# Second-type MLPs: up projections of 18 of 22 pairs as seven products of quarter matrices, with the weight sums made by DMA in the first block

## The chip, the core and the metric

The kernel runs on one core of a Trainium2 chip. The metric is the device time of one execution in microseconds. TensorE (PE) multiplies, with its weight loads shown as PEld; VectorE (DVE), ScalarE (ACT) and GpSimd (POOL) do the elementwise work; SyncE (SP) issues DMAs, and ACT and POOL can issue them too.

## The reference, cut to what matters

A sequence of 512 tokens with 1024 channels goes through one block of a first type and two layers of a second type. The change concerns the MLP that closes each second-type layer:

```python
    for l in range(DEPTH_2):
        ...
        h2 = _rmsnorm(x, g_ffn[l])
        z = _dwconv(h2 @ w_up[l].astype(h2.dtype), w_dw_ffn[l], b_dw_ffn[l])
        zg, zv = jnp.split(z, 2, axis=-1)
        x = x + (jax.nn.silu(zg) * zv) @ w_down[l].astype(h2.dtype)
    return _rmsnorm(x, g_final)
```

w_up is 1024 x 5632 (2816 gate columns, then 2816 value columns), w_down 2816 x 1024; _dwconv is a convolution of three taps over the tokens, for each column by itself.

## The kernel before

**Layout.** x stays on the chip, transposed: 8 tiles of 128 channels x 512 tokens. A projection into 128 output columns is a sum over 8 input tiles. Every fp32 number is used as a high and a low part, so each 128x128 weight block costs three matmuls (mm3, L380 to L382: high x high, high weight x low input, low weight x high input) of 512 columns into one PSUM bank.

**Weights** are packed by the host into units of 8 blocks (512 KB), in the order of use, and streamed by prep and take: a DMA on SP's queue into raw (3 buffers), a cast on ACT into whi (L359), a subtraction on POOL into wlo (L360), 4 buffers each. take starts a unit's chain three units ahead of PE (AHEAD = 3). The engines are in-order queues; the order on each is set by a scheduler, with hand-made queue-order edges through issue_behind.

**The second-type MLP.** 22 pairs (128 gate and 128 value columns) go in two chunks of 11 (CHUNK2). The first four projections of a layer (two pairs) are made "outer": input tile by input tile, as x becomes ready (proj_outer). Behind them fin makes the RMS factor r: a matmul with ones over the squares (total, L480), ACT and DVE steps (rsqrt, L344, L489 to L491). Then each pair takes two PSUM banks of the pool's eight; conv3 multiplies a bank by r (L1289, DVE), starts the conv with a scaled copy (L1292, ACT) and adds two shifted terms (L1293, L1294, DVE); silu (L344, ACT), the product gate x value (L1308, DVE) and the split into ah (L448, ACT) and al (L449, DVE) follow. After a chunk's 11 pairs, 8 down projections of 11 blocks are added to x (L1313, DVE). norm_in, ahead of the MLP, makes xh and xl of x (L451, ACT; L452, DVE) and sums squares (L463).

**The end.** final makes the last two down projections in halves of 256 columns, the last norm (total, L480, and rsqrt) for each half, and the outputs o (L1348, DVE and POOL), each half's as soon as its factor is there.

**The first block** has an attention of eight heads, in which ACT, DVE and PE alternate, then its gates and its own MLP.

## Time and profile before

| | |
|---|---|
| median of 3 runs | 1880.58 us (1879.77 to 1882.03) |
| profiled execution | 1880.29 us, of it span 1878.6 us |
| PE busy | 1839.2 us, 98% of the span |
| DVE, ACT, POOL busy | 958, 946, 938 us (51%, 50%, 50%) |
| second-type MLP, first layer | 923.7 to 1283.4 us |
| second-type MLP, second layer | 1505.7 to 1867 us |

Shares are averages over stages. The chain of waits puts 89% of the span on PE. In the two MLP stages PE never idles; everywhere else its gaps are short.

### The profile page before, as it was taken

How to read it: one execution, taken by the hardware profiler on the slowest of the kernel's cores; microseconds unless marked ns; L12 is line 12 of the kernel's file. 1: busy time of each engine (PE TensorE's matmuls, PEld its weight loads, DVE VectorE, ACT ScalarE, POOL GpSimd, SP SyncE). 2: the span in 40 equal slices, each digit the busy share in tenths (PEclk: the TensorE clock that was granted, in tenths of full speed). 3: DMA queues.
4: the chain of work that ended last, by engine and by line, in shares of the span. 5: the costliest groups of instructions: out<-in, count | busy, mean ns of one | idle time of the engine just before them, and what ended most of it. 6: DMA issues, size and time to landing. Idle time of an engine off the chain costs nothing.

```text
span 1878.6 us, 22097 instructions
## 1 busy us (share of the span) xinstructions
PE 1839.2 (98%) x8448; PEld 1495.8 (80%) x8448; DVE 958.1 (51%) x1420; ACT 946.3 (50%) x1442; POOL 938.4 (50%) x510
## 2 busy tenths in 40 slices
PE   8999999999999999999999999999999999999997
PEld 6877888888888888766888888888866788888886
DVE  4666552724022037997565225522898565405543
ACT  6766633643243347697554224433778554314442
POOL 5233444644444557866644444454966464444442
PEclk9999999999999999999999999999999999999999
DMA  5111223222222222200222222222210122222221
GB/s 188 68 57 62 79 101 135 93 94 101 92 99 98 94 90 71 98 29 21 94 106 95 97 101 91 101 101 90 91 51 23 64 99 101 101 91 101 100 91 56
DMA packets 48649, 164.89 MB, mean 88 GB/s; under 512 B 5536, under 2 KB 7584, under 8 KB 48544
## 3 DMA queue, kind: packets, MB, share of 16 engines
q1 hardware_dynamic: 46304, 160.34, 24.3%
q10 hardware_dynamic: 2240, 3.15, 0.5%
q8 instruction: 66, 1.08, 0.2%
q14 instruction: 39, 0.32, 0.1%
HBM read 161.37 MB, written 2.10 MB: 87 GB/s over the span
## 4 chain that ended last, share of the span: by engine, by line
PE 89%; DVE 6%; ACT 3%; issue 1%; POOL 1%; DMA 0%; SPq 0%; DVEq 0%; ACTq 0%; POOLq 0%
PE b L381 23%; PE b L382 23%; PE b L380 23%; PE mm L381 3%; PE s L1140 3%; PE mm L380 3%; PE mm L382 3%; PE t L1157 2%; DVE xl L452 1%; PE av L1162 1%; PE av L1163 1%; PE cv L480 1%; ACT whi L359 1%; DVE x L650 1%; PE b L480 1%
## 5 line engine op out<-in xcount | busy, mean ns | idle before, releaser
L360 POOL TENSOR_TENSOR wlo<-raw,whi 128x1024 fp32r<-128x1024 f32 x300 | 720.9, 2405 | 809.9 <-ACT whi L359 809.6
L359 ACT CAST whi<-raw 128x1024 fp32r<-128x1024 f32 (+1 forms) x302 | 313.6, 1040 | 506.4 <-PE b L381 414.6
L380 PE MATMUL b<-xh,whi 128*128 128x512 f32 (+1 forms) x1296 | 495.4, 382 | 2.7 <-ACT xh L451 2.7
L381 PE MATMUL b<-xl,whi 128*128 128x512 f32 (+1 forms) x1296 | 491.4, 379 | 3.4 <-DVE xl L452 3.4
L382 PE MATMUL b<-xh,wlo 128*128 128x512 f32 (+1 forms) x1296 | 491.1, 379 | 0.0
L381 PEld LDWEIGHTS b<-xl,whi 128*128 128x128 f32 x1296 | 244.1, 188 | 51.9 <-DVE xl L452 4.2
L380 PEld LDWEIGHTS b<-xh,whi 128*128 128x128 f32 x1296 | 244.2, 188 | 50.5 <-ACT xh L451 3.1
L382 PEld LDWEIGHTS b<-xh,wlo 128*128 128x128 f32 x1296 | 244.1, 188 | 45.6
L380 PE MATMUL b<-ah,whi 128*128 128x512 f32 (+1 forms) x646 | 243.6, 377 | 0.0
L381 PE MATMUL b<-al,whi 128*128 128x512 f32 (+1 forms) x646 | 243.2, 377 | 0.0
L382 PE MATMUL b<-ah,wlo 128*128 128x512 f32 (+1 forms) x646 | 243.2, 376 | 0.0
L381 PEld LDWEIGHTS b<-al,whi 128*128 128x128 f32 x646 | 121.6, 188 | 22.4
L380 PEld LDWEIGHTS b<-ah,whi 128*128 128x128 f32 x646 | 121.5, 188 | 22.4
L382 PEld LDWEIGHTS b<-ah,wlo 128*128 128x128 f32 x646 | 121.6, 188 | 22.0
L1228 POOL TENSOR_TENSOR cacc<-cacc,pd 128x510 f32<-128x510 f32 (+14 forms) x94 | 119.8, 1275 | 26.6 <-ACT pd L1226 22.8
L1212 DVE SCALAR_TENSOR_TENSOR cv<-u,vec,cv 128x497 f32<-128x497 f32 (+13 forms) x146 | 108.2, 741 | 8.4 <-ACT cv L1202 6.5
L1289 DVE TENSOR_TENSOR b<-b,r 128x512 f32<-128x512 f32 x88 | 61.0, 697 | 97.3 <-PE b L382 97.1
L1313 DVE TENSOR_TENSOR x<-x,b 128x512 f32<-128x512 f32 x30 | 20.6, 687 | 161.3 <-PE b L382 161.3
L448 ACT CAST ah<-cg 128x512 fp32r<-128x512 f32 x44 | 27.3, 621 | 98.7 <-DVE cg L1308 98.7
L380 PE MATMUL mm<-xh,whi 128*128 128x512 f32 x176 | 69.3, 394 | 0.0
L871 DVE TENSOR_TENSOR b<-rl,b 128x512 f32<-128x512 f32 x32 | 22.1, 696 | 92.5 <-ACT rl L870 92.5
L381 PE MATMUL mm<-xl,whi 128*128 128x512 f32 x176 | 68.7, 391 | 0.0
(430 smaller groups left out, 2851.0 us busy)
## 6 DMA issues: line engine op xcount, KB each, us to landing
raw<-w SPq DMA_DIRECT2D x295, 512.0 KB, 3.2
x<-xT SPq DMA_DIRECT2D x8, 256.0 KB, 6.5
x<-xT ACTq DMA_DIRECT2D x8, 256.0 KB, 4.8
raw<-w SPq DMA_DIRECT2D x7, 256.0 KB, 2.6
outT<-o ACTq DMA_DIRECT2D x4, 256.0 KB, 2.4
outT<-o SPq DMA_DIRECT2D x4, 256.0 KB, 2.5
vec<-vec SPq DMA_DIRECT2D x1, 363.0 KB, 6.9
f<-pos SPq DMA_DIRECT2D x1, 256.0 KB, 3.3
```

What stands on the lines that cost most here:

```text
L359: nc.scalar.copy(out=hi[:, cs], in_=raw[:, cs])
L360: (eng or nc.gpsimd).tensor_tensor(out=lo[:, cs], in0=raw[:, cs], in1=hi[:, cs].bitcast(F32), op=ALU.subtract)
L380: mm(ps, lhsT=wb[0], rhs=xb[0], start=start, stop=False, **kw)
L381: mm(ps, lhsT=wb[0], rhs=xb[1], start=False, stop=False, **kw)
L382: mm(ps, lhsT=wb[1], rhs=xb[0], start=False, stop=stop, **kw)
L448: nc.scalar.copy(out=hi, in_=src)
L480: self.nc.tensor.matmul(full[:, :n], lhsT=self.ones, rhs=a, start=i == 0, stop=i == len(parts) - 1)
L1140: mm(s, lhsT=q[:, qb * P : (qb + 1) * P], rhs=k, start=True, stop=True)
L1157: nc.tensor.transpose(pt[:, qb * P : (qb + 1) * P], probs[qb][:, t * P : (t + 1) * P], self.ident)
L1212: ins = V.scalar_tensor_tensor(out=acc[:, o], in0=us[i][:, u], scalar=self.v("w_dw_conv_2", l, i * CONV_K + k), in1=acc[:, o], op0=ALU.mul ...
L1228: G.tensor_tensor(out=acc[:, o], in0=acc[:, o], in1=pd, op=ALU.add)
L1289: V.tensor_tensor(out=ps, in0=ps, in1=r, op=ALU.mult)
```

## The change

**Seven products.** Take a pair's 256 x 1024 weights as quarters, gate or value columns against the first or second four input tiles (a11, a12: gate; a21, a22: value), and the normed input as quarters B11, B12, B21, B22: first or second four tiles against the first or second 256 tokens. Pairs 0 to 3 of each layer stay plain; for pairs 4 to 21 the two banks are made of seven products of a weight quarter (or sum S1 to S4) with an input quarter (or difference T1 to T4), each 4 blocks x 3 matmuls of 256 columns, with copies (snap, ACT) and additions (plus, DVE) of half banks between. A pair has 84 matmuls of 256 columns in place of 48 of 512. The value half comes out with its sign turned, for which the conv uses weights negated at the start (wneg).

**Inputs.** quarter_inputs writes the seven input operands once per layer. The norm factor goes into them, so total moves from behind the outer projections to behind their first three input tiles, and pairs 4 to 21 lose their multiply by r. hp, the pool of its temporaries, is closed before the conv tiles' pool is opened.

**Weights.** A new host array wq holds the quarters, rearranged only. S1 to S4 are made on the device in DRAM: 40 copies on ACT's queue and 40 accumulating additions on POOL's, of 1 MB each (0.5 MB for one region in five), issued one or two behind the casts (or the subtractions) of units 8 to 99. In before those units run from 37 to 600 us. In the quarter phase a unit arrives as two or three DMAs instead of one.

**Chunks and end.** Three chunks of 7, 7 and 8 pairs. The last two products of a chunk's last pair are interleaved with its first three down projections. In final, the first half's outputs come behind the second half's factor; those of tiles 4 to 7 on DVE behind the last addition to x.

```diff
-CHUNK2 = 11
+CHUNKS2 = (0, 7, 14, 22)
+PLAIN2 = 4
+OUTER2 = 2
+NDOWN = 3
+SUM_PAIRS = 4
+SUMS = ("S1", "S2", "S3", "S4")
+QUARTERS = ("a11", "a12", "a21", "a22")
+SIDE = {u: 2 if 10 <= u < 27 else 1 if u < 41 or u % 2 else 0 for u in range(8, 120)}
...
+        for _ in range(SIDE.get(u, 0)):
+            if self.side:
+                begin, on_pool = self.side.popleft()
+                self.issue_behind(begin(), rest if on_pool else cast)
...
+        for name, base, more in (("S1", "a21", "a22"), ("S3", "a11", "a21"), ("S2", "S1", "a11"), ("S4", "S2", "a12")):
+            for l in range(NL):
+                for g, r in enumerate(regs):
+                    self.side.append((copy(self.sum_of[l, name, g], self.sum_of[l, base, g] if base in SUMS else quarter(l, base, r)), False))
+            for l in range(NL):
+                for g, r in enumerate(regs):
+                    self.side.append((add(self.sum_of[l, name, g], quarter(l, more, r)), True))
...
+                if k == OUTER_LAG + 2 and between is not None:
+                    between()
...
+        op_ = tc.tile_pool(name="quarters", bufs=1, side="right", reuse_waits="tile")
+        ops = self.quarter_tiles(op_.__enter__())
+        hp_ = tc.tile_pool(name="hp", bufs=1, reuse_waits="tile")
+        hp = hp_.__enter__()
+        rs = []
+        def norms():
+            rs.append(fin(pp, "b", True))
+            self.quarter_inputs(hp, ops, "g_ffn_2", l, rs[0][1])
+        pss = self.proj_outer(pp, "b", acts, 2 * OUTER2, between=norms)
+        pss += [self.proj(pp, "b", acts) for _ in range(2 * (PLAIN2 - OUTER2))]
+        r = rs[0][0]
+        self._close(hp_)
+        self._close(xg)
+        ffc = tc.tile_pool(name="ffc", bufs=max(len(ks) for ks in chunks2()), reuse_waits="tile")
...
+                for f in ks:
+                    if f >= PLAIN2:
+                        break
+                    pg, pv = pss[2 * f : 2 * f + 2]
+                    for ps in (pg, pv):
+                        V.tensor_tensor(out=ps, in0=ps, in1=r, op=ALU.mult)
+                    a.append(unit(f, pg, pv, self.v("w_dw_ffn_2", l, 3 * (NF2 + f), 3)))
+                def snap(ps):
+                    t = fp.tile([P, S // 2], F32, name="snap", bufs=4)
+                    with tc.high_priority():
+                        A.copy(out=t, in_=ps)
+                    return t
+                def plus(out, a, b):
+                    with tc.high_priority():
+                        V.tensor_tensor(out=out, in0=a, in1=b, op=ALU.add)
+                def times(ps, name, start, stop):
+                    hi, lo = ops[name]
+                    for kk in range(KT // 2):
+                        self.mm3(ps, self.take(), (hi[:, kk], lo[:, kk]), start and kk == 0, stop and kk == KT // 2 - 1, skip_group_check=True)
+                def p4(g):
+                    times(g["v"][:, L], "T4", False, True)
+                    plus(g["v"][:, R], g["g"][:, R], g["u3"])
+                def p3(g):
+                    times(g["g"][:, R], "B22", False, True)
+                    plus(g["g"][:, R], g["g"][:, R], g["u2"])
+                    a.append(unit(g["f"], g["g"], g["v"], self.wneg[l][:, 3 * g["f"] : 3 * g["f"] + 3]))
+                old = None
+                for f in ks:
+                    if f < PLAIN2:
+                        continue
+                    g = {"f": f, "v": pp.tile([P, S], F32, name="b"), "g": pp.tile([P, S], F32, name="b")}
+                    times(g["v"][:, L], "B11", True, False)
+                    u1 = snap(g["v"][:, L])
+                    times(g["g"][:, L], "B21", True, True)
+                    plus(g["g"][:, L], g["g"][:, L], u1)
+                    if old is not None:
+                        p4(old)
+                    times(g["v"][:, L], "T2", False, False)
+                    g["u2"] = snap(g["v"][:, L])
+                    times(g["g"][:, R], "T1", False, False)
+                    if old is not None:
+                        p3(old)
+                    times(g["v"][:, L], "T3", False, False)
+                    g["u3"] = snap(g["v"][:, L])
+                    old = g
+                ds = [pp.tile([P, S], F32, name="b") for _ in range(NDOWN)]
+                def down(n0, n1):
+                    for n in range(n0, n1):
+                        k, m = divmod(n, NDOWN)
+                        self.mm3(ds[m], self.take(), a[k], k == 0, k == len(ks) - 1)
+                down(0, 4)
+                p4(old)
+                down(4, 8)
+                p3(old)
+                down(8, NDOWN * len(ks))
+                tail = 2 if l == NL - 1 and c == last_chunk else 0
+                for m in range(KT - tail):
+                    ps = ds[m] if m < NDOWN else self.proj(pp, "b", a)
+                    V.tensor_tensor(out=self.x[m], in0=self.x[m], in1=ps, op=ALU.add)
+                if tail:
+                    self.final(pp, a)
...
+    def quarter_inputs(self, pool, ops, gname, l, r):
+        nc = self.nc
+        V, A, G = nc.vector, nc.scalar, nc.gpsimd
+        L, R = HALVES
+        for k in range(0, KT // 2, 2):
+            h = []
+            for k0 in (k, KT // 2 + k):
+                t = pool.tile([P, 2, S], F32, name=f"h{len(h)}")
+                for j in range(2):
+                    V.scalar_tensor_tensor(out=t[:, j], in0=self.x[k0 + j], scalar=self.v(gname, l, k0 + j), in1=r, op0=ALU.mult, op1=ALU.mult)
+                h.append(t)
+            (b11, b12), (b21, b22) = ((t[:, :, L], t[:, :, R]) for t in h)
+            def put(name, src, eng):
+                hi, lo = (t[:, k : k + 2] for t in ops[name])
+                A.copy(out=hi, in_=src)
+                eng.tensor_tensor(out=lo, in0=src, in1=hi.bitcast(F32), op=ALU.subtract)
+            def temp():
+                return pool.tile([P, 2, S // 2], F32, name="t", bufs=3)
+            put("B11", b11, G)
+            put("B21", b21, G)
+            t1 = temp()
+            V.tensor_tensor(out=t1, in0=b11, in1=b12, op=ALU.subtract)
+            t2 = temp()
+            V.scalar_tensor_tensor(out=t2, in0=t1, scalar=-1.0, in1=b22, op0=ALU.mult, op1=ALU.subtract)
+            put("T2", t2, V)
+            put("T1", t1, V)
+            t3 = temp()
+            V.tensor_tensor(out=t3, in0=b22, in1=b12, op=ALU.subtract)
+            put("T3", t3, V)
+            V.scalar_tensor_tensor(out=t2, in0=t2, scalar=-1.0, in1=b21, op0=ALU.mult, op1=ALU.subtract)
+            put("T4", t2, V)
+            put("B22", b22, G)
...
         def norm(cs):
+            factor(cs)
+            if cs.start:
+                outputs(HALVES[0], added[cs.start])
+                outputs(cs)
...
+                    if behind is not None and j >= KT // 2 and not on_pool:
+                        self.issue_behind(ins, behind)
```

At the end of the plain projections, DVE before and now (b: PSUM banks with their numbers, cg and cv: conv tiles of gate and value, r: the norm factor). Before, where the first layer's MLP begins:

```order
L491 SCALAR_TENSOR_TENSOR r_7992<-b_7993,r_7992 128x512
L1289 TENSOR_TENSOR b_7868<-b_7868,r_7992 128x512
L1289 TENSOR_TENSOR b_7869<-b_7869,r_7992 128x512
L1289 TENSOR_TENSOR b_7870<-b_7870,r_7992 128x512
L1293 SCALAR_TENSOR_TENSOR cg_8002<-b_7868,vec_67,cg_8002 128x511
L1293 SCALAR_TENSOR_TENSOR cv_8007<-b_7869,vec_67,cv_8007 128x511
L1294 SCALAR_TENSOR_TENSOR cg_8002<-b_7868,vec_67,cg_8002 128x511
L1294 SCALAR_TENSOR_TENSOR cv_8007<-b_7869,vec_67,cv_8007 128x511
L1293 SCALAR_TENSOR_TENSOR cg_8019<-b_7870,vec_67,cg_8019 128x511
L1308 TENSOR_TENSOR cg_8002<-cg_8002,cv_8007 128x512
```

Now, at the same layer; b_8011 and b_8012 are pair 0's gate and value, b_8294 is the eighth and last plain bank:

```order
L1439 TENSOR_TENSOR b_8199<-b_8199,r_8063 128x512
L1439 TENSOR_TENSOR b_8230<-b_8230,r_8063 128x512
L1439 TENSOR_TENSOR b_8262<-b_8262,r_8063 128x512
L1439 TENSOR_TENSOR b_8294<-b_8294,r_8063 128x512
L1417 SCALAR_TENSOR_TENSOR cg_8335<-b_8011,vec_67,cg_8335 128x511
L1417 SCALAR_TENSOR_TENSOR cv_8339<-b_8012,vec_67,cv_8339 128x511
L1418 SCALAR_TENSOR_TENSOR cg_8335<-b_8011,vec_67,cg_8335 128x511
L1418 SCALAR_TENSOR_TENSOR cv_8339<-b_8012,vec_67,cv_8339 128x511
L1417 SCALAR_TENSOR_TENSOR cg_8352<-b_8013,vec_67,cg_8352 128x511
L1426 TENSOR_TENSOR b_8011<-b_8011,cv_8339 128x512
L1418 SCALAR_TENSOR_TENSOR cg_8352<-b_8013,vec_67,cg_8352 128x511
L554 TENSOR_TENSOR al_8347<-b_8011,ah_8346 128x512
```

Before, three multiplies stood ahead of the first conv; now all eight multiplies stand ahead of the first conv.

ACT in the same place, before:

```order
L344 ACTIVATE r_7992<-b_7993,epst_122 128x512
L344 ACTIVATE r_7992<-r_7992,lna1024_124 128x512
L340 ACT_TABLE_LOAD
L1292 ACTIVATE cg_8002<-b_7868,vec_67 128x512
L1292 ACTIVATE cv_8007<-b_7869,vec_67 128x512
L1292 ACTIVATE cg_8019<-b_7870,vec_67 128x512
L359 CAST whi_8067<-raw_8066 128x1024
L344 ACTIVATE cg_8002<-cg_8002 128x512
L448 CAST ah_8014<-cg_8002 128x512
```

And now; the casts are of units of the quarter phase, the last of which reuses the whi buffer of the last plain projection:

```order
L406 CAST whi_8232<-raw_8231 128x1024
L1530 CAST T4h_8004<-t_8112 128x512
L406 CAST whi_8264<-raw_8263 128x1024
L406 CAST whi_8296<-raw_8295 128x1024
L406 CAST whi_8401<-raw_8400 128x1024
L1416 ACTIVATE cg_8335<-b_8011,vec_67 128x512
L1416 ACTIVATE cv_8339<-b_8012,vec_67 128x512
L1416 ACTIVATE cg_8352<-b_8013,vec_67 128x512
L1416 ACTIVATE cv_8356<-b_8014,vec_67 128x512
L385 ACTIVATE b_8011<-cg_8335 128x512
L1416 ACTIVATE cg_8368<-b_8199,vec_67 128x512
L553 CAST ah_8346<-b_8011 128x512
```

Four casts of coming units now stand ahead of the first conv's start. On PE, the quarter products follow the eighth plain bank at once; b_8398 and b_8399 are the ninth and tenth bank asked of a pool of eight:

```order
L484 MATMUL b_8294<-xl_7952,whi_8201 128x512
L485 MATMUL b_8294<-xh_7951,wlo_8202 128x512
L483 MATMUL b_8398<-B11h_7994,whi_8232 128x256
L484 MATMUL b_8398<-B11l_7995,whi_8232 128x256
L485 MATMUL b_8398<-B11h_7994,wlo_8233 128x256
L483 MATMUL b_8398<-B11h_7994,whi_8232 128x256
...
L485 MATMUL b_8398<-B11h_7994,wlo_8233 128x256
L483 MATMUL b_8399<-B21h_7996,whi_8232 128x256
```

The norm's total on PE (b<-acc,ones), before, behind the 96 matmuls of the outer projections:

```order
L381 MATMUL b_7871<-xl_7826,whi_7873 128x512
L382 MATMUL b_7871<-xh_7825,wlo_7874 128x512
L480 MATMUL b_7993<-acc_7810,ones_115 128x512
L380 MATMUL b_8034<-xh_7811,whi_7903 128x512
L381 MATMUL b_8034<-xl_7812,whi_7903 128x512
```

Now behind 36 of them (three input tiles x four banks x three):

```order
L484 MATMUL b_8014<-xl_7942,whi_7865 128x512
L485 MATMUL b_8014<-xh_7941,wlo_7866 128x512
L585 MATMUL b_8064<-acc_7936,ones_115 128x512
L483 MATMUL b_8011<-xh_7943,whi_7865 128x512
L484 MATMUL b_8011<-xl_7944,whi_7865 128x512
```

The rows of the other five input tiles now come behind it.

POOL in the first block's attention, before:

```order
L360 TENSOR_TENSOR wlo<-raw,whi 128x1024 x13
L698 COPY pt<-z 128x1
L360 TENSOR_TENSOR wlo<-raw,whi 128x1024 x5
L698 COPY pt<-z 128x1
L698 COPY pt<-pt 128x2
L360 TENSOR_TENSOR wlo<-raw,whi 128x1024 x5
L698 COPY pt<-z 128x1
```

Now, from unit 14 on, the additions of S1 (S_0_0 to S_1_4: layer and region, 1024 rows of 256 elements):

```order
L407 TENSOR_TENSOR wlo<-raw,whi 128x1024 x12
L809 COPY pt<-z 128x1
L452 DMA S_0_0_138<-wq 1024x256
L452 DMA S_0_1_142<-wq 1024x256
L407 TENSOR_TENSOR wlo<-raw,whi 128x1024
L452 DMA S_0_2_146<-wq 1024x256
L452 DMA S_0_3_150<-wq 1024x256
L407 TENSOR_TENSOR wlo<-raw,whi 128x1024
L452 DMA S_0_4_154<-wq 512x256
```

Two additions stand between the low parts of one unit and of the next.

## Rows read from the trace of the kernel before

**Rows 1.** The page: busy time; DMA share (tenths) and GB/s by slice.

```profile
PE 1839.2 (98%) x8448; PEld 1495.8 (80%) x8448; DVE 958.1 (51%) x1420; ACT 946.3 (50%) x1442; POOL 938.4 (50%) x510
...
DMA  5111223222222222200222222222210122222221
...
GB/s 188 68 57 62 79 101 135 93 94 101 92 99 98 94 90 71 98 29 21 94 106 95 97 101 91 101 101 90 91 51 23 64 99 101 101 91 101 100 91 56
```

**Rows 2.** Windows: us, each engine's busy (x instructions), PEclk, DMA share, GB/s.

```profile
923.73:1283.44 359.71, 359.71 (x1586) 297.49 (x1585) 157.75 (x211) 143.09 (x179) 173.03 (x76) 1.00 0.28 97
...
1850.71:1860.66 9.95, 9.95 (x84) 9.95 (x83) 3.07 (x6) 3.21 (x6) 0.00 (x0) 1.00 0.01 2
...
681.19:688.99 7.80, 7.80 (x67) 7.79 (x66) 1.11 (x2) 3.25 (x5) 3.65 (x2) 1.00 0.29 105
```

**Rows 3.** Groups, 930-1280 us: xcount | busy us, mean ns | idle before.

```profile
L359 ACT CAST whi<-raw 128x1024 fp32r<-128x1024 f32 x66 | 69.3, 1052 | 112.6 <-PE b L381 104.9 <-POOL acc L463 6.3 <-issue 1.2
...
L1292 ACT ACTIVATE cg<-b,vec 128x512 f32<-128x512 f32 x22 | 16.9, 770 | 3.3 <-DVE b L1289 3.3
...
L344 ACT ACTIVATE cg<-cg 128x512 f32<-128x512 f32 x22 | 13.9, 632 | 30.5 <-DVE cg L1294 30.5
...
L448 ACT CAST ah<-cg 128x512 fp32r<-128x512 f32 x22 | 13.7, 621 | 49.3 <-DVE cg L1308 49.3
...
L1289 DVE TENSOR_TENSOR b<-b,r 128x512 f32<-128x512 f32 x44 | 30.5, 697 | 48.7 <-PE b L382 48.6
...
L1308 DVE TENSOR_TENSOR cg<-cg,cv 128x512 f32<-128x512 f32 x22 | 18.2, 825 | 0.7
...
L1293 DVE SCALAR_TENSOR_TENSOR cg<-b,vec,cg 128x511 f32<-128x511 f32 x22 | 16.4, 747 | 15.8 <-ACT cg L1292 15.8
...
L449 DVE TENSOR_TENSOR al<-cg,ah 128x512 fp32r<-128x512 f32 x22 | 15.2, 691 | 13.1 <-ACT ah L448 13.1
...
L360 POOL TENSOR_TENSOR wlo<-raw,whi 128x1024 fp32r<-128x1024 f32 x66 | 158.8, 2407 | 183.6 <-ACT whi L359 183.6
```

**Rows 4.** Timelines, that stage's start: start us, us, instruction [idle before].

```profile
919.43 9.67 DVE L452 SCALAR_TENSOR_TENSOR xl<-x,vec,xh 128x512 fp32r<-128x512 f32 x5
...
931.33 0.74 DVE L452 SCALAR_TENSOR_TENSOR xl<-x,vec,xh 128x512 fp32r<-128x512 f32 x1
...
932.00 0.68 DVE L463 TENSOR_TENSOR acc<-acc,sq 128x512 f32<-128x512 f32 x1
...
945.49 1.02 PE L480 MATMUL b<-acc,ones 128*128 128x512 f32 x2
...
949.50 0.69 DVE L491 SCALAR_TENSOR_TENSOR r<-b,r 128x512 f32<-128x512 f32 x1
```

**Rows 5.** Timeline: PE's gap ending the first block; window behind it.

```profile
693.43 0.28 PE L382 MATMUL b<-ah,wlo 128*128 128x256 f32 x1
...
696.03 0.38 PE L380 MATMUL b<-xh,whi 128*128 128x256 f32 x1 [2.32 <-ACT xh L451]
...
697.45 0.39 PE L381 MATMUL b<-xl,whi 128*128 128x256 f32 x1 [1.03 <-DVE xl L452]
...
698.70:702.10 3.40, 3.40 (x14) 0.50 0.29 113
```

**Rows 6.** The page's DMA issues: xcount, KB each, us to landing.

```profile
raw<-w SPq DMA_DIRECT2D x295, 512.0 KB, 3.2
...
raw<-w SPq DMA_DIRECT2D x7, 256.0 KB, 2.6
```

**Rows 7.** Windows in the first block: attention; its MLP.

```profile
82.50:118.40 35.90, 33.89 (x172) 28.32 (x171) 23.76 (x32) 25.53 (x44) 10.26 (x5) 1.00 0.16 59
...
386.60:605.00 218.40, 218.40 (x963) 180.53 (x962) 56.66 (x79) 77.45 (x104) 96.34 (x40) 1.00 0.27 97
```

**Rows 8.** Timelines of the end: outputs on DVE, issues on ACT.

```profile
1864.05 3.19 DVE L1348 TENSOR_TENSOR o<-x,f 128x256 f32<-128x256 f32 x6
...
1872.91 1.63 ACTq L1350 DMA_DIRECT2D outT<-o  x2
```

More of the change, by code (lines that the diff above doesn't have):

```diff
@@ L78, in _span, with chunks2 @@
     return np.arange(c0, c0 + n)
+def chunks2():
+    return [range(a, b) for a, b in zip(CHUNKS2, CHUNKS2[1:])]
 def weight_plan():
@@ new lines, in prep, with sources @@
+        for cs in (slice(*c) for c in cuts):
+            cast = nc.scalar.copy(out=hi[:, cs], in_=raw[:, cs])
+            rest = (eng or nc.gpsimd).tensor_tensor(out=lo[:, cs], in0=raw[:, cs], in1=hi[:, cs].bitcast(F32), op=ALU.subtract)
+        self.units[u] = (hi, lo)
+        for _ in range(SIDE.get(u, 0)):
+            if self.side:
+                begin, on_pool = self.side.popleft()
+                self.issue_behind(begin(), rest if on_pool else cast)
+    def sources(self, u):
+        out = []
+        for b, (name, l, f, kk) in enumerate(self.plan[u]):
+            if name in QUARTERS:
+                src = self.wq[l, QUARTERS.index(name), f - PLAIN2]
+            elif name in SUMS:
+                reg, i = divmod(f - PLAIN2, SUM_PAIRS)
+                src = self.sum_of[l, name, reg].rearrange("r (x c) -> (r x) c", c=KT // 2 * P)[i * P : (i + 1) * P]
+            else:
+                src = None
+            key = (name, f) if src is not None else None
+            if out and out[-1][0] == key:
+                out[-1][2] = b + 1
+            else:
+                out.append([key, b, b + 1, src, kk])
+        res = []
+        for key, b0, b1, src, k0 in out:
+            if key is None:
+                res.append((b0 * P, b1 * P, self.w[u, :, b0 * P : b1 * P]))
+            else:
+                res.append((b0 * P, b1 * P, src[:, k0 * P : (k0 + b1 - b0) * P]))
+        return res
@@ L1375, in arrays @@
         "w": pack_weights(inputs, weight_plan()),
+        "wq": pack_quarters(inputs),
         "vec": pack_vectors(inputs),
```

136 lines of the change are left out of this document (90 added, 46 removed).

## The prediction

> **What bounds the kernel now.** I read the busy shares first: PE is at 98%, no other engine over 51% [rows 1]. The windows then show how that splits: in the first layer's MLP PE is busy 359.71 us of 359.71 at full granted clock [rows 2], so nothing is waited for there, and time can only be won by fewer or shorter matmuls. The groups of that stage price every helper that the change touches [rows 3]; the timeline of its start shows the norm [rows 4]; a gap elsewhere shows what PE loses behind an idle stretch [rows 5]. The reader is to see that before has no wait in this stage that could be removed; each wait that the change adds comes on top.
>
> **What the products save.** One 512-column matmul costs 359.71 us / 1586 = 226.8 ns [rows 2]. For 256 columns the end of the kernel has 84 in 9.95 us, that is 9.95 / 83 spacings = 119.9 ns, and the end of the first block 7.80 / 65 = 120 [rows 2]. A pair goes from 48 x 0.2268 = 10.89 us to 84 x 0.1199 = 10.07, so 36 pairs save 36 x 0.81 = **29.3 us**. Both rows for 256 columns are stretches of 8 to 10 us; the quarter phase holds the pace for over 60 us at a time. In them PEld is as busy as PE (9.95 of 9.95), so that stream has no slack left in the weight loads.
>
> **Can the feeders follow?** A unit of 8 blocks lasts 24 x 0.2268 = 5.44 us now and 24 x 0.1199 = 2.88 us in the quarter phase. POOL's low part takes 2.41 us [rows 3]: 84% of it, which holds if nothing else is on POOL there, and nothing is. ACT has per pair 3.5 casts of 1.05, two conv starts of 0.77, silu 0.63, ah 0.62, three snaps of about 0.4: 7.7 of 10.07 us. DVE: four conv steps of 0.75, product 0.83 at most, al 0.69, four plus of about 0.4: 6.1 us. SP has 2 or 3 issues per unit. A raw buffer is held for landing 3.2 [rows 6] + cast 1.05 + low part 2.41 = 6.7 us, and three buffers give 3 x 2.88 = 8.6 us; behind that the four whi and wlo buffers leave some 3 us more. The stage asks for 512 KB / 2.88 us = 182 GB/s; the first slice of the kernel had 188 at half the DMA share [rows 1]. So I take nothing for the steady state; were landing to rise by over 5 us, each unit would be late.
>
> **The start of the quarter phase** is where I find the largest price. The four plain pairs fill all eight banks, so the first product B11 has to wait until pair 0's convs have read its value bank, and the second, B21, until al has read its gate bank. In the order of DVE all eight multiplies by r come ahead of these convs, the eighth of them on a bank that PE has just finished; on ACT four casts come ahead of the conv starts, the last on a buffer that PE has just released. So the convs of pair 0, whose banks were full long ago, begin only when PE ends the plain phase. From that end: cast to +0.8 (it starts one matmul early), cg to +1.5, four conv steps of 0.75 to +4.6: B11 starts, 12 matmuls, 1.44 us. Then on DVE one more conv step, the product, another step and al, 0.75 + 0.83 + 0.75 + 0.69, to +7.5, where B21 starts instead of +1.44 [rows 3]. **Loss: 6.1 us a layer.** What is late next is nothing: pair 1's banks come free at about +13, when the next pair of banks is wanted.
>
> Behind a gap of 2.32 us and another of 1.03, PE was granted half clock for 3.40 us, with 14 matmuls in it where full clock has 28 [rows 5]: half of 3.40 us lost. The new gaps, 4.6 and 1.4 us, are longer, so I add **1.7 us a layer**; nothing is the other end.
>
> The total moves behind 36 matmuls: 923.73 + 36 x 0.2268 = 931.9. The last sum of squares ends at 932.68 [rows 4]: PE waits **0.9 us a layer**, where before the total at 945.49 waited for nothing.
>
> **The quarter inputs** have to be done by the end of the plain phase, which is 192 matmuls, the wait of 0.9 and the total's two of 0.23, 44.9 us behind the outer start. From the total's start r took 949.50 + 0.69 - 945.49 = 4.7 us [rows 4], so now it is there 932.68 + 4.7 - 923.73 = 13.6 us behind the start: 31.3 us remain. DVE has in them 8 steps from PSUM of 0.75, 8 multiplies of 0.70 (36 of the layer's 44 go [rows 3]), and 16 steps from SBUF alone. For such steps the trace has two prices: 0.74 us with POOL idle, 9.67 / 5 = 1.93 with POOL at work [rows 4]. Sum: 6.0 + 5.6 + 16 x 0.74 = 23.4 us, or with 1.93, 42.5. Following the order of ACT, DVE and POOL by hand with these durations (POOL: six low parts and six half-size subtractions, often waiting for a cast) gives a mean of 1.28 for the 16 and the eighth multiply ends some 1.4 us after the plain phase, just before ACT has the first conv start ready. I take **0.5 us a layer**, with 0 and 11 as ends. The Trainium skill (SBUF — State Buffer, "Who interferes with whom") says that a DVE instruction with two SBUF inputs contends with a GpSimd instruction that reads SBUF, and that whoever comes second blocks until the other has finished. The 1.93 against 0.74 agrees in kind; multiplies from PSUM keep 0.70. By full blocking, these steps would run only while POOL is idle; that is the second rival below.
>
> **Chunk ends.** A chunk's last pair has from its last plus to al about 0.4 + 2 x 0.77 + 2 x 0.75 + 0.63 + 0.83 + 0.62 + 0.69 = 6.2 us [rows 3], up to 6.9 where steps queue. The cover is the first three down projections up to the last k: 10 blocks x 3 x 0.2268 = 6.8 us in chunks of 7. Six chunk ends, 0 to 0.7 us each: I take **1.7 us**.
>
> **The end.** Outputs of the first half now come behind the second factor; before, six of them took 3.19 us on DVE, while the second half's matmuls ran [rows 8]. Part now runs between the last matmul and the last DMA, in DVE's waits for ACT: **+1 us**, between -1 and +3.
>
> **The first block.** ACT issues 40 copies: an issue of ACT took 1.63 / 2 = 0.8 us [rows 8], so 33 us of ACT, 20 of the issues in attention, where ACT is busy 25.5 of 35.9 us [rows 7]. PE there is busy 33.89 of 35.90, so it already waits at times. POOL's 40 additions have no row. Below, an issue costs what ACT's did; above, POOL's idle time bounds it: 5.44 - 2.41 = 3.0 us beside each low part in the MLP with an addition to every second unit (6.1 us), and in attention (35.90 - 10.26) / 4 units = 6.4 us for two. So up to about 3 us each costs PE nothing. Their transfers (1 MB, in rows of 1 KB, read twice and written) have none either; the nearest moves 512 KB in 3.2 us [rows 6], so some 6.4 us a MB, and they are followed by one each 11 us. Nothing downstream needs the sums before 970 us. I take **3 us**, mostly for ACT in attention, with 0 and 40 as ends.
>
> **Sum:** 1880.29 - 29.3 + 2 x (6.1 + 1.7 + 0.9 + 0.5) + 1.7 + 1.0 + 3.0 = 1875.1 for the profiled execution, which lies 0.3 us under the median of the runs shown: **1875.4 us**, 0.28% faster.
>
> **The rivals.**
> *A: the additions block POOL (slower).* Should an addition hold POOL for more than 5 us, or its transfer last over 11 us so that the queue of POOL stands still until an earlier one has landed, low parts behind it are late and PE waits. At 8 us, attention's 20 lose (8 - 3.2) x 20 = 96 us less what the three units of lead take once (some 15 us a burst, two bursts): about +65; the MLP's 20 lose 8 - 6.1, about +38. At 6 us it is about a quarter. For it: nothing like it is in the trace, and 1 KB rows are short. Against: 6.4 us by the nearest transfer, and POOL's idle time. From 5 us on it decides; time 1890 to 1980. The Trainium skill (DMA: Bandwidth & Descriptors, "SWDGE vs HWDGE vs iDMA") says that accumulating is only possible on GpSimd's path, where a program on GpSimd computes each descriptor; its fit for that path, 2.0 us + bytes / 436e3, would give an estimated 4.4 us for 1 MB, so no loss. No run here shows it. **0.11.**
> *B: the quarter inputs are late (slower).* If the 16 steps only run while POOL is idle, DVE needs 23.4 us plus POOL's 6 x 2.41 + 6 x 1.2 = 21.7, together 45.1 against 31.3 + 1.4: up to 12.4 us late a layer, 1875.4 + 2 x 12 = 1899. It decides from a mean of (32.7 - 11.6) / 16 = 1.32 us a step; at 1.5 it is 3 us a layer, 1881. **0.10.**
> *C: the feeders don't follow (no change).* With ACT's casts queued behind snaps that wait for PE, POOL at 84% loses its 0.47 us a unit now and then: 0.3 us for each of 36 pairs give 1875 + 11 = 1886, 0.1 give 1879; or 256-column pace 122 ns over long stretches, 3024 x 2 ns = 6 us, 1881. **0.20.**
> *D: the start costs little (faster).* No half clock, and the end of the plain phase not exposed: 1875.4 - 2 x 6 = 1863. **0.15.**
>
> **How the numbers follow.** The forecast itself, with its bounds, 1868 to 1880, has 0.44; two thirds of it lie under 1876.8. About 0.2% (3.8 us) is what a measurement of this kernel can tell from no change: under 1876.8 is faster, over 1884.3 slower. Faster: 0.30 of the forecast, all of D, a fifth of C, 0.49. Slower: A, six tenths of B, a third of C, 0.23. The rest is 0.28. Range 1860 to 1893: it takes in D, C and the cheaper parts of A and B.
>
> **What would show it.** Right: 256-column matmuls 120 ns apart in both quarter phases with no idle; before the first product of each layer an idle of about 4.6 us released by a conv step on DVE, then 1.4 by al, and half clock behind. The total waits 0.9 us for acc. In the first block the low parts keep their 5.44 us spacing. Wrong: PE waiting for wlo in the quarter phase (C), for wlo or a cast in attention (A), a first idle of over 6 us with DVE in steps of 1.5 us or more ahead of it (B), or none (D).

## The result, and the profile after

The changed kernel takes 1960.2 us (median of 4 runs, 1959.9 to 1966.8) against 1880.2 us: 1.0432 times the time before, 95% interval 1.0409 to 1.0455, so some 80 us slower where 5 us less was forecast. The profiled execution is the longest of the four, 1966.8 us (span 1965.1); differences between traces below are against it, 86.5 us over the one before.

The page of the changed kernel: busy time, then PE and PE's granted clock in 40 slices of 49 us.

```profile
PE 1833.9 (93%) x9726; PEld 1536.4 (78%) x9726; DVE 1022.9 (52%) x1520; ACT 1043.7 (53%) x1634; POOL 1134.8 (58%) x618
...
PE   8973966998999999999999999999999999999997
...
PEclk9996987999999999999999999999999999999999
```

PE's work is 5.3 us shorter than before, but its share fell from 98% to 93%. The digits say where: PE falls to 7 and 3 in slices 3 and 4 and to 6 in slices 6 and 7, between 98 and 344 us, in the first block's attention; the granted clock falls there too. Behind that PE is nearly full. The same is read from one row, the matmul behind the gap that ends the first block, here in the changed kernel:

```profile
797.59 0.38 PE L483 MATMUL b<-xh,whi 128*128 128x256 f32 x1 [2.32 <-ACT xh L556]
```

Before, this matmul started at 696.03 [rows 5]. So the first block is **101.6 us longer**, and everything behind it is 101.6 - 86.5 = **15.1 us shorter** (the forecast without its term for the first block has 8.2 there). Who made PE wait, in the changed kernel (us in total, times, longest):

```profile
PE av L793 <- DVE plzC L785: 40.2, 3, 38.7
PE b L483 <- ACT dh L553: 20.8, 1, 20.8
PE b L483 <- ACT b L385: 9.0, 2, 4.5
PE b L484 <- DVE xl L557: 8.4, 5, 5.1
PE b L484 <- DVE dl L554: 6.6, 1, 6.6
```

Three waits (38.7, 20.8, 6.6 us) stand in attention; the two of 4.5 us are the starts of the quarter phases. To see what lies behind the longest, the changed kernel's POOL from 124 us on (L452 issues an addition, L407 is the low part of a unit, L809 a copy of a column that a step of DVE, L808, needs):

```profile
124.69 1.30 POOL L452 DMA_DIRECT2D S<-wq  x1 [7.96 <-issue]
125.48 2.94 POOL L407 TENSOR_TENSOR wlo<-raw,whi 128x1024 fp32r<-128x1024 f32 x1
127.84 1.56 POOL L452 DMA_DIRECT2D S<-wq  x1
134.80 1.28 POOL L452 DMA_DIRECT2D S<-wq  x1 [5.40 <-issue]
135.58 2.87 POOL L407 TENSOR_TENSOR wlo<-raw,whi 128x1024 fp32r<-128x1024 f32 x1
152.32 1.30 POOL L452 DMA_DIRECT2D S<-wq  x1 [13.87 <-issue]
161.81 1.29 POOL L452 DMA_DIRECT2D S<-wq  x1 [8.19 <-issue]
162.58 2.87 POOL L407 TENSOR_TENSOR wlo<-raw,whi 128x1024 fp32r<-128x1024 f32 x1
172.53 2.35 POOL L452 DMA_DIRECT2D S<-wq  x2 [7.08 <-issue]
173.95 1.12 POOL L809 COPY pt<-z 128x1 f32<-128x1 f32 x1
```

And DVE, then PE, at the end of that stretch:

```profile
175.10 0.69 DVE L808 TENSOR_TENSOR pt<-pt 128x510 f32<-128x510 f32 x1 [41.44 <-POOL pt L809]
175.71 0.69 DVE L785 TENSOR_TENSOR plzC<-pt,phzC 128x512 fp32r<-128x512 f32 x1
```

```profile
176.45 0.58 PE L793 MATMUL av<-plzC,v 128*128 128x256 f32 x1 [38.67 <-DVE plzC L785]
```

An issue itself is 1.3 us long. Yet POOL stands idle ("issue": for nothing that the profile shows) 5 to 14 us before most of them go out, with low parts and copies queued behind. Only the one at 127.84, 3.15 us after its predecessor, and the second of the two at 172.53 went without a pause: these are themselves the additions of half size (512 rows), so that one and a half were under way. The sum of these pauses over the whole kernel, and what the DMA engines did from 130 to 180 us (busy share in tenths, slices of 1.25 us):

```profile
POOL S L452 <- issue: 125.2, 19, 13.9
```

```profile
DMA  9999989909359999200499994007999990029999
```

The engines fall idle at 151, 161 and 171 us, and within 1.5 us of each of these the next issue starts (152.32, 161.81, 172.53): POOL goes on when the transfer ahead has drained. The column copy, 1 us of work, comes at 173.95; DVE waited 41.4 us for it, and PE, for plzC on DVE, 38.7 us. The granted clock then was 0.50, the lower level of 1.2 GHz, from 141.3 to 182.3 us behind PE's idling, and again for 30.7 us from 284.7; PE stayed at half speed into the work that followed.

### The profile page after: what moved, and what is told of

It reads as the page before. It is cut to its first block, busy times and chain, and to the rows that moved or that the text cites. A ratio compares the mean times of both kernels' runs of the same rounds, so it can differ in the third digit from the quotient of the medians.

```text
span 1965.1 us, 25729 instructions
## 1 busy us (share of the span) xinstructions
PE 1833.9 (93%) x9726; PEld 1536.4 (78%) x9726; DVE 1022.9 (52%) x1520; ACT 1043.7 (53%) x1634; POOL 1134.8 (58%) x618
## 3 DMA queue, kind: packets, MB, share of 16 engines
q8 instruction: 76, 1.25, 0.2%
## 5 line engine op out<-in xcount | busy, mean ns | idle before, releaser
L407 POOL TENSOR_TENSOR wlo<-raw,whi 128x1024 fp32r<-128x1024 f32 (+1 forms) x354 | 857.5, 2431 | 564.3 <-ACT whi L406 560.9
L406 ACT CAST whi<-raw 128x1024 fp32r<-128x1024 f32 (+1 forms) x356 | 370.1, 1042 | 495.3 <-PE b L484 348.7
L484 PE MATMUL b<-xl,whi 128*128 128x512 f32 (+1 forms) x720 | 270.4, 376 | 8.4 <-DVE xl L557 8.4
L483 PE MATMUL b<-xh,whi 128*128 128x512 f32 (+1 forms) x720 | 274.0, 381 | 2.7 <-ACT xh L556 2.7
L485 PE MATMUL b<-xh,wlo 128*128 128x512 f32 (+1 forms) x720 | 269.6, 374 | 1.1 <-POOL wlo L407 1.1
L484 PEld LDWEIGHTS b<-xl,whi 128*128 128x128 f32 x720 | 136.1, 189 | 37.6 <-DVE xl L557 9.6
L483 PEld LDWEIGHTS b<-xh,whi 128*128 128x128 f32 x720 | 136.2, 189 | 31.2 <-ACT xh L556 3.1
L485 PEld LDWEIGHTS b<-xh,wlo 128*128 128x128 f32 x720 | 136.2, 189 | 27.8 <-POOL wlo L407 1.6
L452 POOL DMA_DIRECT2D S<-wq x40 | 51.9, 1310 | 146.1 <-issue 125.2
L557 DVE SCALAR_TENSOR_TENSOR xl<-x,vec,xh 128x256 fp32r<-128x256 f32 (+1 forms) x56 | 70.3, 1267 | 6.6 <-ACT xh L556 6.6
L554 DVE TENSOR_TENSOR al<-b,ah 128x512 fp32r<-128x512 f32 x76 | 52.3, 690 | 40.8 <-ACT ah L553 40.7
L982 DVE TENSOR_TENSOR b<-rl,b 128x512 f32<-128x512 f32 x32 | 22.1, 696 | 97.6 <-ACT rl L981 97.6
## 6 DMA issues: line engine op xcount, KB each, us to landing
S<-wq POOLq DMA_DIRECT2D x32, 1024.0 KB, 10.5
```

What stands on the lines that cost most here:

```text
L406: cast = nc.scalar.copy(out=hi[:, cs], in_=raw[:, cs])
L407: rest = (eng or nc.gpsimd).tensor_tensor(out=lo[:, cs], in0=raw[:, cs], in1=hi[:, cs].bitcast(F32), op=ALU.subtract)
L452: return lambda: nc.gpsimd.dma_start(out=dst, in_=src, accum_op=ALU.add, max_dma_last_dim=row)
L483: mm(ps, lhsT=wb[0], rhs=xb[0], start=start, stop=False, **kw)
L484: mm(ps, lhsT=wb[0], rhs=xb[1], start=False, stop=False, **kw)
L485: mm(ps, lhsT=wb[1], rhs=xb[0], start=False, stop=stop, **kw)
```

## The experiments

Each experiment was timed once, e9 and e11 four times. "Late" is the end of the first block against before, from the start of that 2.32 us gap (693.7 us before).

| kernel | time, us | first block late, us |
|---|---|---|
| before / after | 1880.2 / 1960.2 | 0 / 101.6 |
| e1: a larger store for POOL's DMAs | 1894.3 | 30.5 |
| e2: no additions | 1881.5 | 22.4 |
| e3: additions from unit 41 on | 1906.3 | 44.4 |
| e4: additions in rows of 4 KB | 1892.4 | 28.8 |
| e5: before, tiles moved by 576 B | 1892.3 | 6.8 |
| e6: after, tiles moved by 448 B more | 1964.2 | 93.9 |
| e7: e4 and the 448 B | 1891.9 | 22.1 |
| e8: e2 and the 448 B | 1888.3 | 20.0 |
| e9: copies and additions spread anew | 1855.5 | -0.4 |
| e10: neither copies nor additions | 1857.7 | -0.5 |
| e11: e9, own buffers for pair 0 | 1844.0 | -1.0 |
| e12: before, tiles moved by 256 B | 1880.2 | 0.0 |

**What holds POOL's queue.** The theory: the kernel gives POOL's DMA path a store of 4096 bytes (dynamic_dma_scratch_size); an addition of 1024 rows fills over half of it, so each issue stands until the one ahead has drained. Rivals: the transfers themselves are too slow, or DVE and PE lose to shared memory or DMA traffic. e1 doubles the store, e2 leaves the additions out, e3 puts them behind attention, e4 makes a quarter of the rows of the same bytes.

```diff
-..., num_devices=1, dynamic_dma_scratch_size=4096)
+..., num_devices=1, dynamic_dma_scratch_size=8192)
```

> POOL's descriptor store for its DMAs is doubled from 4096 to 8192 bytes, nothing else. Theory R (the store holds about 1.5 additions of 1024 rows, so POOL stands at the next addition until the one before it has drained, about 10 us): room for about three additions, so each burst of ten loses about two waits of 10 us and the two stalls of 38.7 and 27 us shrink by about half: 1915 to 1940 us. Theory B (the DMA engines are saturated and weights come late, whoever waits): no change, 1955 to 1965 us.

1894.3 us, better than the 1915 to 1940 expected. DMA issues (KB, median us from issue to landing, that is until the data is written) of e1, then what is left of POOL's pauses, then the same column copy, which now runs at 133.53:

```profile
S<-wq POOLq DMA_DIRECT2D x32, 1024.0 KB, 14.5
```

```profile
POOL S L452 <- issue: 8.1, 4, 4.9
```

```profile
133.53 0.45 POOL L809 COPY pt<-z 128x1 f32<-128x1 f32 x1 [0.55 <-DVE plzA L785]
```

The additions land later than in the changed kernel (14.5 us against 10.5), and 66 us are back all the same: not the transfer's length, but how many fit into the queue's store, held PE.

```diff
-            for l in range(NL):
-                for g, r in enumerate(regs):
-                    self.side.append((add(self.sum_of[l, name, g], quarter(l, more, r)), True))
```

> The 40 additions on POOL are left out (S1 to S4 are then plain copies, so the products are of other numbers); the 40 copies stay. Theory R: block 1 ends where it did before the change, at 694 us give or take 4, and the rest keeps its gain of 15 us: 1862 to 1869 us. Theory C (the copies on ACT's queue, 33 us of issue time, share in the loss): 1880 us or more, with block 1 ending at 710 or later.

1881.5 us, by the branch of theory C: 79 us of the result hang on the additions. But the first block is still 22 us late without any, so they are not the whole of it. (Without the additions in the list the copies move up: all 40 are issued by 236 us, where the changed kernel has issued 20.)

```diff
-SIDE: copies, then additions, up to two per unit from unit 8 on
+copies: S1 u8-17, S3 u18-27 (one a unit), S2 u52-70, S4 u72-90 (even)
+additions: every second unit, u41-59 S1, u61-79 S2, u81-99 S4, u101-119 S3
```

> All copies and additions stay, but the additions come behind every second unit from unit 41 to 119, none in the attention; the first 20 copies come behind units 8 to 27. Theory R: with one addition per 10.9 us and about 10.3 us to drain one, POOL's queue hardly stands, no stall of over 7 us is left: 1863 to 1872 us. Theory B (the additions' traffic itself slows PE's weights by its volume): the loss only moves into the MLP, 1900 us or more.

1906.3 us, a miss of over 30. In the MLP's spacing of 10.9 us the additions landed in 13.4 us (median), so POOL's queue stood there too, and the low parts behind it were late (POOL's pauses, and waits of PE, of e3):

```profile
POOL S L450 <- issue: 132.1, 17, 11.7
```

```profile
PE b L487 <- POOL wlo L407: 14.1, 6, 4.5
```

So the store is a limit in the MLP as well. The queue stood as long as in the changed kernel (132 us against 125) and cost less than half; by the rows above, what makes attention dear is that POOL's small copies there lead through DVE to PE at once.

```diff
-nc.gpsimd.dma_start(out=dst, in_=src, accum_op=ALU.add, max_dma_last_dim=row)
+nc.gpsimd.dma_start(out=dst, in_=src, accum_op=ALU.add, max_dma_last_dim=4 * row)
```

> The additions in rows of 1024 elements (4 KB) instead of 256, so 256 rows a MB; order and places as in the changed kernel. Theory R, in which the count of rows fills the store: six additions fit, POOL hardly ever stands, 1865 to 1885 us, whether or not a transfer gets shorter. Theory T (a transfer of 1 MB takes 10 us and the next waits for it, whatever its rows): 1950 to 1965 us.

1892.4 us, 7 us over the expected range. The additions land in 10.8 us, as before the edit, POOL has no pause before any of them, and it issues two in a row and goes on (POOL in e4):

```profile
99.00 2.39 POOL L407 TENSOR_TENSOR wlo<-raw,whi 128x1024 fp32r<-128x1024 f32 x1 [5.23 <-ACT whi L406]
101.33 1.78 POOL L452 DMA_DIRECT2D S<-wq  x2
```

Fewer rows or a larger store do the same, with the same bytes moved and no shorter landing; so it was not the transfers, nor their traffic, that held POOL. That the store holds an entry for each row is inferred from these two, not seen in a record. The low part at 99.00 now waits for its cast, as it should.

**The moved tiles.** wneg, 576 bytes a partition, stands ahead of the weight buffers and moves them, while the normed inputs lie at the other end of the memory and stay. In the changed kernel matmuls of 512 columns on these inputs follow each other at 233 ns (the first block's MLP; three from row to row, 0.70 us), where before has 226.8 [rows 2]:

```profile
499.63 0.39 PE L483 MATMUL b<-xh,whi 128*128 128x512 f32 x1
...
500.33 0.39 PE L483 MATMUL b<-xh,whi 128*128 128x512 f32 x1
```

e5 adds only such a shift to before, e6 rounds the shift of the changed kernel up to 1024 bytes, e7 and e8 do so with e4 and e2, and e12 adds 256 bytes to before.

```diff
 (e5, before)
+        for j in range(2):
+            nc.gpsimd.memset(c.tile([P, 66], F32, name=f"pad{j}"), 0.0)
 (e12, before)
+            nc.gpsimd.memset(c.tile([P, 64], F32, name="pad0"), 0.0)
 (e6, after; the same in e7 and e8)
+        nc.gpsimd.memset(c.tile([P, 112], F32, name="pad"), 0.0)
```

> The kernel before with 576 bytes per partition reserved (two small tiles set to zero once on POOL) where the change puts its negated conv weights, nothing else. Theory A (where input tiles stand at the right end of SBUF, which don't move, their distance to the weights is no longer a multiple of 512 bytes, and a matmul of 512 columns then goes at 233.3 ns in place of 226.7): the stages with such inputs, some 4000 matmuls, lose 6.6 ns each, 1880 + 25 = 1900 to 1910 us, all at the same PE busy share. Theory D (the 233.3 ns come from the DMA traffic or the new instructions of the change): no change, 1879 to 1882 us.

> The changed kernel with 448 bytes more reserved behind the negated conv weights, so that all tiles behind move by 1024 bytes in sum, not 576. Theory A: 226.7 ns again in the attention, the gates, the up projections of the first block and the mixers, 25 us less, but the quarter inputs at the right end then stand as in the kernel before and their matmuls go back from about 117.5 to 119.9 ns, 7 us more: 1935 to 1948 us with the long stalls in the attention unchanged. Theory D: 1955 to 1965 us.

> Additions in rows of 4 KB and the 448 bytes. If the two causes (POOL's queue held by the additions, and the pace by address) add up: 1892 - 18 = 1870 to 1878 us, faster than the kernel before. If the pace only filled time in which PE would have waited anyway: 1885 to 1892 us.

> The additions left out (the sums are plain copies), the 40 copies kept, and the 448 bytes. Theory A with the copies costing little: 1881.5 - 18 = 1860 to 1867 us, block 1 ending at 694 to 700 us. If the copies on ACT's queue have a price of their own, block 1 ends later than 700 us and the time is 1868 to 1880.

> The kernel before with 256 bytes per partition reserved at the left of the weight buffers (576 in e5_before_shift, which took 12 us). If only a distance of a multiple of 512 bytes between the weights and the input tile goes at 226.7 ns: again 1888 to 1896 us, with 512-column matmuls slower than 226.7 ns in the stages with inputs at the right end. If a multiple of 64, 128 or 256 is enough, the distance of 256 goes as before: 1879 to 1882 us; since 576 is a multiple of 64, only 128 or 256 could be the rule then.

e5: 1892.3 us, 12 us more for nothing but addresses, half of what was expected; e12: 1880.2, nothing. e6 missed theory A's range by 16 us, e8 both of its branches by 8 us and more, and e7 fell into its second by number alone; the reason is below. Windows of 60 us in the first block's MLP (columns as in [rows 2]), of before, of e5 and of e12:

```profile
535.00:595.00 60.00, 60.00 (x266) 49.71 (x265) 15.26 (x22) 23.63 (x34) 26.41 (x11) 1.00 0.27 97
```

```profile
541.00:601.00 60.00, 60.00 (x258) 48.32 (x258) 14.80 (x22) 22.34 (x32) 25.49 (x11) 1.00 0.29 96
```

```profile
541.00:601.00 60.00, 60.00 (x267) 49.69 (x266) 15.26 (x22) 23.59 (x34) 26.59 (x12) 1.00 0.29 97
```

PE is busy all 60 us at full clock in each, but e5 gets 258 matmuls done instead of 266. e6 has the 512-column pace of before again and its first block is 7.7 us shorter than after's; e7's is 6.7 shorter than e4's, e8's 2.4 shorter than e2's. Yet the totals of e6 to e8 do not fall (e8 is 6.8 us above e2), because the matmuls of 256 columns go the other way. Windows in the second chunk's quarter products of the first layer, of the changed kernel, of e6, of e9 (which has the 448 bytes and 64 more behind the quarter inputs), and of e2 (no tile moved against the changed kernel):

```profile
1150.00:1210.00 60.00, 59.74 (x506) 59.55 (x507) 28.78 (x48) 39.33 (x60) 50.06 (x22) 1.00 0.55 179
```

```profile
1145.00:1205.00 60.00, 59.83 (x499) 59.62 (x498) 29.38 (x49) 39.51 (x62) 49.84 (x21) 1.00 0.59 182
```

```profile
1045.00:1105.00 60.00, 60.00 (x528) 59.70 (x527) 29.74 (x49) 41.11 (x63) 51.49 (x22) 1.00 0.60 186
```

```profile
1068.00:1128.00 60.00, 60.00 (x527) 59.70 (x526) 29.09 (x48) 40.87 (x62) 50.52 (x22) 1.00 0.59 185
```

That is about 118, 120, 114 and 114 ns a matmul. The shift of 1024 bytes alone gives 120 ns in all six chunks of e6, e7 and e8. Without it, or with the 64 bytes more, a chunk has 114 or 118 ns: in the changed kernel the first chunk of a layer has 114 and the other two 118, in e2 and e9 the second has 114. So e9's 114 here is not shown to come of its 64 bytes; they bring it back from 120, and what decides between 114 and 118 stays open. From row to row the quarter products of both layers add up to 358 us in the changed kernel, 367 in e6, 355 in e9 and 352 in e2. In the changed kernel as it stands the two effects of the shift about cancel; e9 has the better of both.

**The remaining 20 us.** Without POOL's block and at the old pace, e7 is still 22 us late. By the casts of the units around 34, behind attention, e8 (40 copies on ACT's queue, no additions) is 20 us late, e4 (20 copies and 20 additions by then, two a unit) 16 to 21, e3 (20 copies, one a unit, no additions yet) 7 to 8. So copies issued by ACT in attention cost something; that additions two a unit do too is suggested by e4 against e3, not shown. e10 has neither copies nor additions, to see whether anything else is in it. e9 keeps both and moves them: the 20 copies of S1 and S3 on SP's queue, one a unit from unit 8 on, S2 and S4 on ACT's behind attention, the additions one a unit (u14 to 33) and then one every second (u61 to 99), in rows of 4 KB.

```diff
+("S1", "a21", "a22", "SP", range(8, 18), range(14, 24)),
+("S3", "a11", "a21", "SP", range(18, 28), range(24, 34)),
+("S2", "S1", "a11", "ACT", (*range(42, 52, 2), *range(60, 70, 2)), range(61, 81, 2)),
+("S4", "S2", "a12", "ACT", range(66, 86, 2), range(81, 101, 2)),
```

> The changed kernel with what the earlier runs point to: the 20 copies for S1 and S3 on SP's queue, one a unit (8 to 27), those for S2 and S4 on ACT behind units 42 to 84, outside the attention; additions in rows of 4 KB, one a unit from 14 to 33 and one every second unit from 61 to 99; 448 bytes at the left and 64 at the right end of SBUF, so that the 512-column inputs stand at a multiple of 512 bytes from the weights and the quarter inputs don't. If POOL's queue, ACT's issues in the attention and the two paces are all of the loss: block 1 ends within 4 us of the kernel before (694 to 698 us) and the whole is 1857 to 1864 us. If copies cost PE by their traffic and not by ACT's time: block 1 ends at 705 to 712 us, 1868 to 1878 us.

> No copies and no additions at all (the sums are read as plain quarters, so the products are of other numbers; weights arrive in the same pieces), with the same two paddings. This is the change without its side traffic: block 1 as before the change, 693 to 696 us; quarter phases with the 4.5 and 1.4 us waits at their start: 1854 to 1860 us.

e9: 1855.5 us, 0.9865 times before (95% interval 0.9848 to 0.9881), 1.5 us under its range; e10: 1857.7, within. The first block's end in e9 (e10's row stands at 695.49):

```profile
695.66 0.49 PE L489 MATMUL b<-xh,whi 128*128 128x256 f32 x1 [2.32 <-ACT xh L562]
```

So the sums can all be made in the first block for nothing; the 20 us were where and how closely the issues stood (e9 changes queue, spacing and place together), not what they move. The copies on ACT are shown as a cause (e8, which has nothing else); how much of the 20 us in the changed kernel is theirs, and how much the additions', two a unit, is not separated. Part of e8's 20 us is clock: in four stretches between 79 and 185 us, 17 us in all, its granted clock is 0.50, where e10 has full clock from 12 to 697 us; by the 16.2 us that PE is busy in them, an estimated 8 us. An issue is only 0.5 us of ACT, but the order in which ACT and DVE run differs between e8 and e10 at some 20 places on each as well, between e9 and e10 at 3 and 2, so that this may be the issues' time or the order: that stays open.

**The start of the quarter phase.** In e9 the two waits of 4.5 us remain. The conv tiles of pair 0 come from a pool that is opened when the plain inputs' pool is closed, so they may have to wait for memory that is in use until the plain phase's last matmul. e11 gives pair 0 its own four tiles (beside the quarter inputs) and emits it, with priority, right behind the outer projections.

```diff
+        ep_ = tc.tile_pool(name="early", bufs=1, side="right", reuse_waits="tile")
...
+        with tc.high_priority():
+            first = plain(0, ep)
         pss += [self.proj(pp, "b", acts) for _ in range(2 * (PLAIN2 - OUTER2))]
```

> As e9_respread, and pair 0 of each layer's MLP has tiles of its own for its conv and its two halves, so that it needn't wait until the inputs of the plain projections are given up: its two banks are free when the plain phase ends. If the wait at the start of the quarter phase comes from that order: the idle of 4.5 and 1.4 us a layer and the half clock behind go, 2 x 6 to 9 us less than e9_respread. If DVE, which has the quarter inputs to make in the same time, is the limit: they come later by the 6 us of pair 0's conv, and the time stays within 3 us of e9_respread.

1844.0 us (1842.4 to 1849.7), **0.9811 times before (0.9795 to 0.9827)**, 11.5 us under e9 (12 to 18 were expected; the two profiled executions are 14.6 apart) and the fastest of all. Its paces are those of e9 (527 and 528 matmuls in 60 us of the second chunk), so the new tiles brought nothing that way. DVE in e11 has that conv and its split during the plain phase:

```profile
949.81 0.73 DVE L1421 SCALAR_TENSOR_TENSOR cg<-b,vec,cg 128x511 f32<-128x511 f32 x1
...
954.43 0.69 DVE L560 TENSOR_TENSOR al<-b,ah 128x512 fp32r<-128x512 f32 x1
```

and PE crosses the border with no idle at full clock (window of e11):

```profile
963.00:1000.00 37.00, 37.00 (x284) 35.27 (x283) 29.19 (x47) 28.84 (x45) 31.76 (x13) 1.00 0.53 171
```

e11 changes memory, place and priority at once; which of the three was needed is not separated.

## Why the prediction was wrong

**The step that failed is "The first block": 3 us, with 40 as its upper end, measured 101.6.** By the runs it splits into about 71 us for POOL's queue (e1: 101.6 to 30.5; e4: 73), 7 for the moved tiles (e5, e6, e7), and some 22 for copies and additions at their places in attention (e7, which e9 brought to nothing). Three things went wrong in that step.

- It bounded what an addition costs POOL by its issue and its transfer. The issue was right (1.3 us, within its 0.8 to 3), the transfer low (10.5 us landing, 6.4 forecast), but neither was the price: the queue stood for its predecessor, 125 us in all, with no more than one and a half additions in flight. Rival A had the direction, a range (1890 to 1980) that holds the result, and the effect, POOL held for over 5 us by an addition. Its second condition was off: it wanted transfers of over 11 us, and it happened at 10.5, by the store and not by the transfer (in e1 the queue hardly stands at 14.5). Its sign, PE waiting for a low part or a cast in attention, hardly came (1.1 us for a low part); PE waited for DVE, behind POOL's column copy. It got 0.11 where nothing in the trace bounded it; "no row" was taken for small.
- It asked only what stands behind an addition among the low parts, with three units of lead. POOL's `COPY pt<-z` stood in the order right beside the additions, and DVE and PE are behind them without any lead. That was readable beforehand.
- It took 3 us for the copies, since ACT has idle time in attention; with POOL's block gone, copies and additions still cost some 20.

The fit that the prediction took from the Trainium skill ("DMA: Bandwidth & Descriptors", where it stands in "Anatomy of one DMA — SWDGE (gpsimd) path") gives an estimated 4.4 us for 1 MB. For these accumulating transfers 10.5 was measured, so the trace differs, and the measurement decides.

**Outside the first block** the forecast's terms, against the changed kernel:

| step | forecast | measured |
|---|---|---|
| wait for the first product, a layer | 4.6, then 1.5 for al | 4.49, then 0 |
| half clock behind it | 1.7 | 3.1 |
| wait for the total, a layer | 0.9 | 0.4 |
| quarter inputs late, a layer | 0.5 | 0 |
| chunk ends, in all | 1.7 | 0 (0.3 at one chunk's start) |
| the end | 1 | 0.8 |
| pace of 256 columns, ns | 119.9 | 114 to 118 (120 in e6) |

The start's first wait went as worked out, step by step. PE, then DVE, then the clock in the changed kernel:

```profile
1077.23 0.55 PE L483 MATMUL b<-B11h,whi 128*128 128x256 f32 x1 [4.49 <-ACT b L385]
```

```profile
1072.78 0.70 DVE L1439 TENSOR_TENSOR b<-b,r 128x512 f32<-128x512 f32 x1 [0.35 <-PE b L485]
1074.36 0.75 DVE L1417 SCALAR_TENSOR_TENSOR cg<-b,vec,cg 128x511 f32<-128x511 f32 x1 [0.88 <-ACT cg L1416]
...
1076.35 0.74 DVE L1418 SCALAR_TENSOR_TENSOR cv<-b,vec,cv 128x511 f32<-128x511 f32 x1
...
1079.00 0.69 DVE L554 TENSOR_TENSOR al<-b,ah 128x512 fp32r<-128x512 f32 x1
```

```profile
1076.60:1083.40 6.80, 6.17 (x29) 6.20 (x30) 5.66 (x10) 4.95 (x8) 0.94 (x1) 0.50 0.42 147
```

Eight multiplies, then the convs, then 4.5 us of idle PE. (The row names ACT's silu, which ended within 0.1 us of pair 0's last conv step on DVE.) The second wait did not show, because the first product ran at half clock and took twice as long, until al was there: 29 matmuls in 6.17 us, half of which (3.1) is lost. In sum 4.5 + 3.1 = 7.6 us a layer against 7.8; that the sum agrees so well is luck, since the idle was 1.6 shorter and the half clock 1.4 dearer than forecast. Whether the reuse of memory, which e11 removed, held the convs besides the order of DVE and ACT is not shown, since e11 moved the order too.

Rivals B (late inputs) and C (feeders) did not occur: in the quarter phases, behind their first product, PE waits for nothing but a snap, 0.3 us. Rival D (a cheap start) is what e11 made, at 1844 where D had 1863.

With e6, which has the paces that the forecast was made with, all behind the first block takes 1964.2 - 787.6 = 1176.6 us against 1880.2 - 693.7 = 1186.5 before: 9.9 us less where 8.2 was forecast. So the sum of the other terms was right to 2 us at these paces; the table's terms came out some 4 us cheaper together, of which some 2 us were lost elsewhere, unexplained. It is not the forecast of what the idea can give: without its first-block term it says 1872.4, and e9, which loses nothing there, takes 1855.5 and lies under the whole range. Behind the first block e9's profiled execution is 13 us shorter than e6, of which 12 are the quarter phases' pace (367 against 355 us): the pace, taken as fixed at 119.9 ns, was the second term that was off.

## What to carry to other kernels

Before DMAs go onto an engine's queue, look up how many the queue's store takes, and then who waits, through one or two other engines, for the smallest instruction behind them; a lead of some units protects only what runs with that lead. An operation that the trace has no row for needs an upper end from what it could block, not from its own length. Where a change moves tiles in memory, compare the pace of untouched matmuls first.
